# VectorE's share of every dense step queued behind the dot of the latest gather, in issue order alone

## The chip, the cores and the metric

The kernel runs on one core of a Trainium2 chip. The metric is the device time of one execution in microseconds, as the median of several runs. The core has a matrix engine (TensorE, rows call it PE), a vector engine (VectorE, DVE), an engine for activation functions (ScalarE, ACT), GpSimd (POOL), which here only issues the gathers, and a queue engine (SyncE, SP), which here issues all plain loads. 16 DMA engines move the data of all queues.

## The reference, cut to what matters

Two layers over one sequence of 512 tokens with 1024 features. Each layer first mixes tokens, then looks up experts:

```
m  = x @ w_in                                  # q, k, v, LRU branch, gates
ya = DiffAttention(q, k, v); yr = RG-LRU(conv4(xr)) * gelu(gr)
x  = LayerNorm(alpha * x + (g0 * (ya @ w_br_attn) + g1 * (yr @ w_br_lru)) @ w_out)
q  = x @ peer_wq                               # 8 heads, two halves each
s  = q . subkeys;  top 16 of 128 in each half; top 16 of the sums -> 16 expert numbers e per head
act = gelu(x . peer_u[e]);  x = LayerNorm(alpha * x + sum_e g[e] * act[e] * peer_v[e])
```

So every token fetches 8 x 16 = 128 experts per layer, each with a row of `peer_u` and a row of `peer_v`.

## The kernel before

**Tiling.** The 512 tokens are four blocks of 128, one token per partition. The host puts `peer_u` and `peer_v` side by side, so that one expert is a row of 2048 floats. A *gather* (line 819) is one indirect DMA by POOL that brings one expert for each of the 128 tokens of a block: a tile `uvt` of 128x2048 floats, 1.05 MB. A block needs 128 gathers, and there are 2 layers x 4 blocks x 128 = 1024. They land in 8 buffers (pool `gather`).

**What each gather needs (`experts`).** VectorE multiplies the first half of `uvt` with the block's rows `xn` and sums: the *dot* (line 822, one instruction of 128x1024 with an accumulator). For each pair of gathers ScalarE takes the GELU of two dots (`q`, line 829) and VectorE multiplies by the routing weights (`w`, line 784). Then the second half of `uvt`, scaled by `w`, is added to the block's sum: either by VectorE (`acc`, line 790) or by ScalarE and TensorE (a diagonal matrix `dg`, line 794, and two matmuls into `pv`, line 796). Which of the two is settled for each gather when the program is written, by an account of each engine's load (`Load`); 346 of the 1024 go to VectorE. Only after that sum is the buffer free for the gather eight places later.

**Dense work.** Everything else is written by two more streams, `dense()` and `late()`. The list `PLAN` has four entries, each for two blocks of a layer: (layer 0, blocks 0 and 1), (layer 0, blocks 2 and 3), (layer 1, blocks 0 and 1), (layer 1, blocks 2 and 3). An entry has a *mixer* (projections, attention, LRU, merges, output projection, layer norm) and then a *route* (`route`, line 673): scores for 16 half-heads (`score`), the top 16 of each for both blocks (`top16`, lines 716 to 721, VectorE alone), and the choice of 16 experts per head (`choose`, lines 723 to 771, nearly all VectorE) for the first of the two blocks. The choices for the second block come in `late()` (`route_late`, line 697). `choose` works on groups of two heads and ends with the write of 32 columns of expert numbers (`e`, line 761), which the gathers of those heads need.

**The order in which it is written.** `run` (line 841) takes one step at a time from the stream that lies furthest back, on a scale counted in gathers: `PLAN` says that, for example, the route of (layer 1, blocks 2 and 3) is to be written between gathers 730 and 786 and the late choices between 786 and 880. A stream can also wait for another (`wants`): a gather is not written before its route, and a mixer of layer 1 not before its blocks' experts.

**The order in which it is issued.** The program is traced in this written order, but a list scheduler then sets the order on each engine: among the instructions of an engine that it holds for ready, the one written earlier goes first; where that one is not ready by its reckoning, a later one goes ahead. Each engine then executes its own list strictly in that order. So dense work on VectorE can be issued many gathers ahead of the place at which it was written.

Of the kernel before, what the change touches and what calls it, by code (L numbers as in the profile page):

```python
# [18 lines left out]
ALU = mybir.AluOpType  # L19
# [3 lines left out]
D = 1024  # L23
# [97 lines left out]
class Decoder:  # L121
# [652 lines left out]
    def experts(self, l, b, G=2):  # L774
        nc, pp = self.nc, self.pp
        x = self.xn[b]
        pv = None
        e, g = self.e[b], self.g[b]
        began = [False]

        def finish(j0, q, uvs):

            w = pp.tile([P, G], F32, name="w", tag="w")
            nc.vector.tensor_tensor(w, q, g[:, j0 : j0 + G], ALU.mult)  # L784
            for i in range(G):
                j, t = j0 + i, uvs[i]
                self.load.update()
                vector = self.load.dve + 1.22 <= self.load.pe + 1.72
                if j == P - 1 or (vector and j < P - 2):
                    nc.vector.scalar_tensor_tensor(out=acc, in0=t[:, D:], scalar=w[:, i : i + 1],  # L790
                                                   in1=acc, op0=ALU.mult, op1=ALU.add)
                else:
                    dg = pp.tile([P, P], F32, name="dg", tag="dg")
                    nc.scalar.activation(dg, self.ident, AF.Copy, scale=w[:, i : i + 1])  # L794
                    for half in range(2):
                        nc.tensor.matmul(pv[:, half], dg,  # L796
                                         t[:, D + half * 512 : D + (half + 1) * 512],
                                         start=not began[0], stop=j == P - 2)
                    began[0] = True
            yield  # L800

        prev = iter(())
        for j0 in range(0, P, G):
            if j0 % TOPK == 0:
                yield ("route", l, b, j0 // TOPK)
                if j0 == 0:
                    if (l, b) == (0, 0):
                        self.load.update()
                        self.load.begin()
                    acc = pp.tile([P, D], F32, name="acc", tag="acc", bufs=1)  # L810
                    nc.scalar.activation(acc, x, AF.Copy, scale=ALPHA)
                    pv = self.ps_v.tile([P, 2, 512], F32, name="pv", tag="pv")
            dots = pp.tile([P, G], F32, name="dots", tag="dots")
            q = pp.tile([P, G], F32, name="q", tag="q")
            uvs = []
            for i in range(G):
                j = j0 + i
                t = self.gp.tile([P, 2 * D], F32, name="uvt", tag="uv")
                nc.gpsimd.indirect_dma_start(  # L819
                    out=t, out_offset=None, in_=self.uv,  # L820
                    in_offset=bass.IndirectOffsetOnAxis(ap=e[:, j : j + 1], axis=0))
                nc.vector.scalar_tensor_tensor(out=t[:, :D], in0=t[:, :D], scalar=1.0, in1=x,  # L822
                                               op0=ALU.mult, op1=ALU.mult,
                                               accum_out=dots[:, i : i + 1])
                uvs.append(t)
                if i == 0:
                    next(prev, None)
                else:
                    nc.scalar.activation(q, dots, AF.Gelu_apprx_tanh)  # L829
                yield 1  # L830
            prev = finish(j0, q, uvs)
        for _ in prev:
            pass
        sums = pp.tile([P, 1], F32, name="sums2", tag="sums2")
        nc.vector.scalar_tensor_tensor(out=x, in0=acc, scalar=1.0,
                                       in1=pv.rearrange("p a c -> p (a c)"), op0=ALU.mult,
                                       op1=ALU.add, accum_out=sums)
        self.layer_norm(l, 1, [(b, sums)], LN_EPS, acc)
        self.done.add(("experts", l, b))

    def run(self):
        nc = self.nc
        self.setup()
        self.cst = [None] * DEPTH
        self.done = set()
        self.load = Load(nc)

        def gathers():
            for l in range(DEPTH):
                for b in range(NB):  # L850
                    yield from self.experts(l, b)
# [28 lines left out]
        streams = [gathers(), dense(), late()]  # L880
# [3 lines left out]
        while any(live):  # L884
            free = [i for i in range(3) if live[i] and (wants[i] is None or wants[i] in self.done)]
            i = min(free, key=lambda i: (at[i], -i))
            wants[i] = None
            c = next(streams[i], None)
            if c is None:
                live[i] = False  # L890
            elif isinstance(c, tuple):
                wants[i] = c
            elif i:
                at[i] = c
            else:
                at[0] += c
# [34 lines left out]
```

## Time and profile before

| | us |
|---|---|
| median of 3 runs (3443.23 to 3445.84) | 3445.73 |
| the profiled execution, its own time | 3443.5 |
| its span, first to last instruction | 3441.3 |
| first gather issued (line 819) | 300.1 |
| last dot starts (line 822) | 3422.2 |
| PE busy | 2962.3 |
| VectorE busy | 2660.9 |
| ACT busy | 1242.6 |

The first 300 us are the mixer and the first route of layer 0, blocks 0 and 1; nothing is gathered there. Then all 1024 gathers follow, with the rest of the dense work beside them. 1285.92 MB are read in all, 1073.81 MB of them by the gathers. The rate at which the DMA engines move data, in GB/s per stretch of the span, is the line to read first; beside it stand the busy time of each engine and the granted clock of TensorE (PEclk, as a share of full speed).

### The profile page before, as it was taken

To read this page: it belongs to the slowest core of one execution; us is meant where nothing else is said; L and a number is where in the kernel's file an instruction comes from. 1 tells how busy PE (TensorE), PEld (TensorE's weight loads), DVE (VectorE), ACT (ScalarE), POOL (GpSimd) and SP (SyncE) were. 2 spreads that over 40 slices of the span, in tenths; PEclk is the share of its full clock that TensorE was granted. 3 is DMA by queue.
4 is the path that set the end of the run, shared out by engine and by line. 5 is a ranking of instruction groups with operands and counts; after the bars stand their busy time and mean duration, and the time that the engine had idled before them with its cause. 6 is when DMAs were issued, how large, how long until landed. Compare 5 with 4: busy or idle time off the path is not lost.

```text
span 3441.3 us, 38208 instructions
## 1 busy us (share of the span) xinstructions
PE 2962.3 (86%) x11832; PEld 1899.5 (55%) x11832; DVE 2660.9 (77%) x6622; ACT 1242.6 (36%) x2851; POOL 1307.3 (38%) x1033
## 2 busy tenths in 40 slices
PE   8997999999997899999996799999998687656655
PEld 8896666777763466677763366666755232212111
DVE  7765989887689577867699569777679965777776
ACT  7852356652122364633122236644122221111111
POOL 0001334444333434434333433433433344565553
PEclk9998999999999999999997999999999799877677
DMA  5455899999999999999998999999999899999997
GB/s 202 155 174 204 332 408 397 414 418 418 418 398 354 380 392 401 393 417 412 418 389 342 412 393 391 401 413 419 418 412 353 312 405 421 421 422 410 421 422 317
DMA packets 219114, 1290.54 MB, mean 375 GB/s; under 512 B 24593, under 2 KB 37137, under 8 KB 87841
## 3 DMA queue, kind: packets, MB, share of 16 engines
q0 software_dynamic: 147456, 1073.81, 77.0%
q1 hardware_dynamic: 71456, 214.30, 16.4%
q8 instruction: 96, 1.57, 0.2%
q14 instruction: 106, 0.86, 0.1%
HBM read 1285.92 MB, written 2.10 MB: 374 GB/s over the span
## 4 chain that ended last, share of the span: by engine, by line
PE 44%; DVE 24%; DMA 19%; issue 6%; POOL 3%; ACT 3%; POOLq 0%; SPq 0%; DVEq 0%; ACTq 0%
DMA uvt<-uv_dram,e 19%; PE ps_mm L253 18%; PE pv L796 16%; DVE uvt L822 8%; POOL uvt L819 3%; DVE acc L790 3%; PE ps_mm L275 3%; PE ps_ln L313 1%; PE ps_qk L253 1%; DVE oh L756 1%; DVE ef L758 1%; PE s L386 1%; DVE oh L753 1%; PE ps_mm L656 1%; PE po L417 1%
## 5 line engine op out<-in xcount | busy, mean ns | idle before, releaser
L819 POOL DMA_INDIRECT uvt<-uv_dram,e x1024 | 1304.7, 1274 | 2101.5 <-PE pv L796 655.1
L796 PE MATMUL pv<-uvt,dg 128*128 128x512 f32 x2712 | 1417.4, 662 | 379.3 <-ACT dg L794 377.8
L822 DVE SCALAR_TENSOR_TENSOR uvt<-uvt,xn 128x1024 f32<-128x1024 f32 x1024 | 1243.8, 1220 | 248.3 <-DMA uvt<-uv_dram,e 244.4
L796 PEld LDWEIGHTS pv<-uvt,dg 128*128 128x128 f32 x2712 | 527.8, 206 | 1094.7 <-ACT dg L794 604.4
L253 PE MATMUL ps_mm<-room_xT,w 128*128 128x256 f32 x2304 | 538.6, 380 | 0.7 <-ACT room_xT L285 0.7
L829 ACT ACTIVATE q<-dots 128x2 f32<-128x2 f32 x512 | 104.1, 203 | 1132.3 <-DVE uvt L822 1117.4
L253 PEld LDWEIGHTS ps_mm<-room_xT,w 128*128 128x128 f32 x2304 | 430.4, 190 | 108.8 <-issue 53.9
L790 DVE SCALAR_TENSOR_TENSOR acc<-uvt,w,acc 128x1024 f32<-128x1024 f32 x346 | 443.6, 1282 | 7.9
L794 ACT ACTIVATE dg<-ident,w 128x128 f32<-128x128 f32 x678 | 257.4, 398 | 290.3 <-DVE w L784 171.1
L784 DVE TENSOR_TENSOR w<-q,g 128x2 f32<-128x2 f32 x512 | 80.7, 158 | 208.9 <-ACT q L829 203.9
L656 PE MATMUL ps_mm<-room_xT,w 128*128 128x256 f32 (+1 forms) x1056 | 241.5, 377 | 0.0
L656 PEld LDWEIGHTS ps_mm<-room_xT,w 128*128 128x128 f32 x1056 | 194.7, 194 | 42.7 <-issue 19.9
L829 ACT ACT_TABLE_LOAD x115 | 147.5, 1283 | 19.6 <-DVE uvt L822 17.0
L238 DVE TENSOR_TENSOR wsp<-raw,wsp 128x1024 fp32r<-128x1024 f32 x80 | 97.1, 1222 | 27.0 <-ACT wsp L237 24.8
L275 PEld LDWEIGHTS ps_mm<-w,room_xT 128*128 128x128 f32 x768 | 90.8, 192 | 8.5 <-issue 7.1
L275 PEld LDWEIGHTS ps_mm<-w,room_m 128*128 128x128 f32 x768 | 89.2, 192 | 9.2 <-issue 8.4
L275 PE MATMUL ps_mm<-w,room_xT 128*128 128x128 f32 x768 | 92.6, 275 | 0.0
L253 PE MATMUL ps_mm<-room_yr,w 128*128 128x256 f32 x384 | 90.1, 380 | 0.0
L253 PE MATMUL ps_mm<-room_ya,w 128*128 128x256 f32 x384 | 89.5, 379 | 0.0
L275 PE MATMUL ps_mm<-w,room_m 128*128 128x128 f32 x768 | 89.3, 275 | 0.0
L237 ACT CAST wsp<-raw 128x1024 fp32r<-128x1024 f32 x80 | 82.7, 1052 | 14.8 <-PE ps_mm L253 7.8
L822 DVE DVE_READ_ACCUMULATOR uvt<-uvt,xn 128x1 f32 x1024 | 84.1, 82 | 0.0
(196 smaller groups left out, 2980.7 us busy)
## 6 DMA issues: line engine op xcount, KB each, us to landing
w<-wpk_dram SPq DMA_DIRECT2D x304, 512.0 KB
raw<-wpk_dram SPq DMA_DIRECT2D x80, 512.0 KB
uvt<-uv_dram,e POOLq DMA_INDIRECT x1024
gw<-gpk_dram SPq DMA_DIRECT2D x32, 128.0 KB
sk<-spk_dram SPq DMA_DIRECT2D x64, 64.0 KB
xn<-x_dram SPq DMA_DIRECT2D x4, 512.0 KB
out_dram<-xn SPq DMA_DIRECT2D x8, 256.0 KB
lq<-lqk_dram SPq DMA_DIRECT2D x2, 128.0 KB
```

The costliest lines, as they stand in the source:

```text
L237: self.nc.scalar.copy(hi, raw)
L238: self.nc.vector.tensor_tensor(lo, raw, hi.bitcast(F32), ALU.subtract)
L253: self.nc.tensor.matmul(ps[:, :n], w, x, start=i == 0, stop=i == len(steps) - 1)
L275: self.nc.tensor.matmul(out[:, i], x(slice(i * P, (i + 1) * P)), w, start=j == 0, stop=j == len(steps) - 1)
L656: nc.tensor.matmul(pq[:, :n], w[:, kc, :], self.acts_x.plain[:, kc, t0 : t0 + n], start=kc == 0, stop=kc == KC - 1)
L784: nc.vector.tensor_tensor(w, q, g[:, j0 : j0 + G], ALU.mult)
L790: nc.vector.scalar_tensor_tensor(out=acc, in0=t[:, D:], scalar=w[:, i : i + 1], in1=acc, op0=ALU.mult, op1=ALU.add)
L794: nc.scalar.activation(dg, self.ident, AF.Copy, scale=w[:, i : i + 1])
L796: nc.tensor.matmul(pv[:, half], dg, t[:, D + half * 512 : D + (half + 1) * 512], start=not began[0], stop=j == P - 2)
L819: nc.gpsimd.indirect_dma_start(out=t, out_offset=None, in_=self.uv, in_offset=bass.IndirectOffsetOnAxis(ap=e[:, j : j + 1], axis=0))
L822: nc.vector.scalar_tensor_tensor(out=t[:, :D], in0=t[:, :D], scalar=1.0, in1=x, op0=ALU.mult, op1=ALU.mult, accum_out=dots[:, i : i + 1])
L829: nc.scalar.activation(q, dots, AF.Gelu_apprx_tanh)
```

## The change

The dot's instruction is kept in `self.dot`, so that it always names the dot of the last gather written so far. When `run` takes a step from `dense()` or `late()`, it does so inside `issue_after(self.dot)`: every VectorE instruction that the step writes may be issued only after that dot has been issued. It is a matter of order on VectorE's list alone: no semaphore, no wait for the dot to finish, nothing on the other engines. Before the first gather there is no dot, and nothing is tied. The gathers' own stream (dots, `w`, `acc`, the layer norm behind the experts) is not tied either. The written order, the choice between `acc` and `pv` and all arithmetic are the same.

```diff
--- before.py
+++ after.py
@@ -819,9 +819,9 @@
                 nc.gpsimd.indirect_dma_start(
                     out=t, out_offset=None, in_=self.uv,
                     in_offset=bass.IndirectOffsetOnAxis(ap=e[:, j : j + 1], axis=0))
-                nc.vector.scalar_tensor_tensor(out=t[:, :D], in0=t[:, :D], scalar=1.0, in1=x,
-                                               op0=ALU.mult, op1=ALU.mult,
-                                               accum_out=dots[:, i : i + 1])
+                self.dot = nc.vector.scalar_tensor_tensor(
+                    out=t[:, :D], in0=t[:, :D], scalar=1.0, in1=x, op0=ALU.mult, op1=ALU.mult,
+                    accum_out=dots[:, i : i + 1]).ins
                 uvs.append(t)
                 if i == 0:
                     next(prev, None)
@@ -843,6 +843,7 @@
         self.setup()
         self.cst = [None] * DEPTH
         self.done = set()
+        self.dot = None
         self.load = Load(nc)
 
         def gathers():
@@ -885,7 +886,12 @@
             free = [i for i in range(3) if live[i] and (wants[i] is None or wants[i] in self.done)]
             i = min(free, key=lambda i: (at[i], -i))
             wants[i] = None
-            c = next(streams[i], None)
+            if i and self.dot is not None:
+
+                with self.tc.issue_after(self.dot):
+                    c = next(streams[i], None)
+            else:
+                c = next(streams[i], None)
             if c is None:
                 live[i] = False
             elif isinstance(c, tuple):
```

What that does to VectorE's list can be counted in dots. In the list of before, the dense instructions of each route stand 20 to 48 dots ahead of the place at which they were written (late ones of the last entry 56 to 100), those of the mixers of the last three entries mostly 4 to 17; in the new list all dense instructions stand 0 to 6 dots behind it. In the first mixer that runs beside gathers (written at gathers 32 to 150), the two lists hardly differ: there before is 0 to 3 dots ahead on average. The four writes of `e` in a route stand behind these dots:

| route of | before | with the change | first gather that needs it |
|---|---|---|---|
| layer 0, block 2 | 211, 223, 233, 241 | 234, 245, 256, 267 | 256, 288, 320, 352 |
| layer 1, block 0 | 448, 457, 469, 479 | 484, 497, 510, 523 | 512, 544, 576, 608 |
| layer 1, block 2 | 708, 719, 730, 740 | 744, 757, 770, 783 | 768, 800, 832, 864 |
| layer 1, block 3 (late) | 744, 749, 753, 757 | 802, 820, 839, 857 | 896, 928, 960, 992 |

The order of POOL's gathers and of SP's loads is the same, but for the place of two stores among the loads. TensorE's and ScalarE's lists change in many places, since the scheduler reckons with the later VectorE work.

VectorE before, at dots 711 and 712, where the route of layer 1, blocks 2 and 3 is issued (`sv`, `si`, `top`: the values and places of the top 16; `sc`: scores; `xn_103` and `g_113`: rows and weights of block 1, whose gathers run here):

```order
L822 SCALAR_TENSOR_TENSOR uvt,dots<-uvt,xn_103 128x1024
L716 MAX sv<-sc 128x8
L716 MAX top_17922<-sc 128x8
L718 MAX_INDEX si<-sv,sc 128x8
L718 MAX_INDEX top_17923<-top_17922,sc 128x8
L721 MATCH_REPLACE sc<-sv,sc 128x128
L822 SCALAR_TENSOR_TENSOR uvt,dots<-uvt,xn_103 128x1024
L716 MAX sv<-sc 128x8
L721 MATCH_REPLACE sc<-top_17922,sc 128x128
L784 TENSOR_TENSOR w<-q,g_113 128x2
L718 MAX_INDEX si<-sv,sc 128x8
L790 SCALAR_TENSOR_TENSOR acc<-uvt,w,acc 128x1024
```

With the change the same gathers have this around them, row after row, from dot 711 on:

```order
L822 SCALAR_TENSOR_TENSOR uvt,dots<-uvt,xn_103 128x1024 x2
L784 TENSOR_TENSOR w<-q,g_113 128x2
L790 SCALAR_TENSOR_TENSOR acc<-uvt,w,acc 128x1024
L822 SCALAR_TENSOR_TENSOR uvt,dots<-uvt,xn_103 128x1024 x2
L784 TENSOR_TENSOR w<-q,g_113 128x2
L790 SCALAR_TENSOR_TENSOR acc<-uvt,w,acc 128x1024
L822 SCALAR_TENSOR_TENSOR uvt,dots<-uvt,xn_103 128x1024 x2
L784 TENSOR_TENSOR w<-q,g_113 128x2
L790 SCALAR_TENSOR_TENSOR acc<-uvt,w,acc 128x1024
L822 SCALAR_TENSOR_TENSOR uvt,dots<-uvt,xn_103 128x1024 x2
L784 TENSOR_TENSOR w<-q,g_113 128x2
```

The steps of the route have left the stretch between these dots: between two dots only `w` and `acc` of the gathers themselves are left.

VectorE before, in the late choices of layer 1, block 3, at dots 746 to 749 (`oh`, `ef`: the one-hot product that looks up the chosen expert's number; `e_111`: expert numbers of block 3):

```order
L753 TENSOR_TENSOR oh<-iota,pf 128x864 x2
L822 SCALAR_TENSOR_TENSOR uvt,dots<-uvt,xn_103 128x1024
L784 TENSOR_TENSOR w<-q,g_113 128x2
L756 TENSOR_TENSOR oh<-oh,ca 128x864 x2
L822 SCALAR_TENSOR_TENSOR uvt,dots<-uvt,xn_103 128x1024
L758 TENSOR_REDUCE ef<-oh 128x16
L784 TENSOR_TENSOR w<-q,g_113 128x2
L758 TENSOR_REDUCE ef<-oh 128x16
L822 SCALAR_TENSOR_TENSOR uvt,dots<-uvt,xn_103 128x1024
L761 CAST e_111<-ef 128x32
```

With the change the same steps stand in the gathers of block 2 (`xn_4375`, `g_114`), at dots 797 to 802:

```order
L753 TENSOR_TENSOR oh<-iota,pf 128x864
L822 SCALAR_TENSOR_TENSOR uvt,dots<-uvt,xn_4375 128x1024
L784 TENSOR_TENSOR w<-q,g_114 128x2
L822 SCALAR_TENSOR_TENSOR uvt,dots<-uvt,xn_4375 128x1024
L756 TENSOR_TENSOR oh<-oh,ca 128x864
L822 SCALAR_TENSOR_TENSOR uvt,dots<-uvt,xn_4375 128x1024
L784 TENSOR_TENSOR w<-q,g_114 128x2
L822 SCALAR_TENSOR_TENSOR uvt,dots<-uvt,xn_4375 128x1024
L758 TENSOR_REDUCE ef<-oh 128x16
L822 SCALAR_TENSOR_TENSOR uvt,dots<-uvt,xn_4375 128x1024
L761 CAST e_111<-ef 128x32
```

A choice of two heads lay within four or five dots; now each of its large steps has a dot or two to itself, and a whole choice has 18.

## Rows read from the trace of the kernel before

**Rows 1.** Page, part 2: GB/s in 40 equal slices of the span.

```profile
GB/s 202 155 174 204 332 408 397 414 418 418 418 398 354 380 392 401 393 417 412 418 389 342 412 393 391 401 413 419 418 412 353 312 405 421 421 422 410 421 422 317
```

**Rows 2.** Stretches: us, busy (instructions) of each engine, PEclk, DMA share, GB/s.

```profile
core 0: us, PE busy (x) PEld busy (x) DVE busy (x) ACT busy (x) POOL busy (x), PEclk, DMA share, GB/s
...
946.00:1204.00 258.00, 216.87 (x673) 123.06 (x672) 208.93 (x695) 72.51 (x192) 98.83 (x80) 0.93 0.96 377
1204.00:1462.00 258.00, 248.26 (x980) 162.94 (x980) 200.39 (x519) 156.37 (x330) 99.18 (x80) 0.97 0.99 395
...
1720.00:1892.00 172.00, 136.73 (x455) 82.21 (x454) 166.33 (x600) 41.74 (x120) 64.55 (x50) 0.89 0.94 366
...
2064.00:2322.00 258.00, 253.67 (x1092) 173.34 (x1091) 214.53 (x471) 154.74 (x317) 102.17 (x84) 1.00 1.00 402
...
2580.00:2752.00 172.00, 122.87 (x347) 64.81 (x346) 171.90 (x618) 45.67 (x115) 61.83 (x50) 0.87 0.90 332
...
2838.00:3354.00 516.00, 320.38 (x503) 106.72 (x501) 372.17 (x607) 73.26 (x232) 286.30 (x206) 0.79 1.01 420
```

**Rows 3.** Waits of PE, then of POOL, 2580 to 2752 us: total us, times, longest.

```profile
PE pv L796 <- ACT dg L794: 44.6, 19, 5.4
...
POOL uvt L819 <- PE pv L796: 38.1, 16, 6.3
```

**Rows 4.** VectorE's groups by line, 2580 to 2752 us: busy us, mean ns.

```profile
L822 DVE SCALAR_TENSOR_TENSOR uvt<-uvt,xn 128x1024 f32<-128x1024 f32 x52 | 63.0, 1212 | 0.0
L790 DVE SCALAR_TENSOR_TENSOR acc<-uvt,w,acc 128x1024 f32<-128x1024 f32 x14 | 17.8, 1272 | 0.0
```

**Rows 5.** The gathers' own instructions on VectorE, whole run: busy us, mean ns.

```profile
L822 DVE SCALAR_TENSOR_TENSOR uvt<-uvt,xn 128x1024 f32<-128x1024 f32 x1024 | 1243.8, 1220 | 248.3 <-DMA uvt<-uv_dram,e 244.4 <-PE pv L796 2.8 <-issue 0.2
...
L822 DVE DVE_READ_ACCUMULATOR uvt<-uvt,xn 128x1 f32 x1024 | 84.1, 82 | 0.0
L784 DVE TENSOR_TENSOR w<-q,g 128x2 f32<-128x2 f32 x512 | 80.7, 158 | 208.9 <-ACT q L829 203.9 <-issue 3.3 <-ACT dg L794 1.3
```

**Rows 6.** A route's instructions on VectorE, whole run, by shape: busy us, mean ns.

```profile
L758 DVE TENSOR_REDUCE ef<-oh 128x16 f32<-128x864 f32 x64 | 66.5, 1045 | 0.1
L753 DVE TENSOR_TENSOR oh<-iota,pf 128x864 f32<-128x864 f32 x64 | 66.4, 1052 | 1.3 <-PE po L417 1.0
L718 DVE FIND_INDEX8 si<-sv,sc 128x8 uint32<-128x128 f32 x128 | 35.8, 283 | 0.0
L716 DVE MAX8 sv<-sc 128x8 f32<-128x128 f32 x128 | 34.7, 282 | 25.4 <-ACT sc L670 23.7 <-ACT dg L794 1.0 <-issue 0.6
L718 DVE FIND_INDEX8 pi<-tv,ca 128x8 uint32<-128x54 f32 x128 | 25.5, 208 | 0.0
L716 DVE MAX8 tv<-ca 128x8 f32<-128x54 f32 x128 | 22.4, 205 | 0.0
L721 DVE MATCH_REPLACE8 sc<-sv,sc 128x128 f32<-128x128 f32 x64 | 17.3, 273 | 0.0
L721 DVE MATCH_REPLACE8 ca<-tv,ca 128x54 f32<-128x54 f32 x64 | 12.3, 199 | 0.0
L736 DVE TENSOR_TENSOR ca<-fi 128x16 f32<-128x16 f32 x64 | 10.8, 169 | 0.0
L718 DVE MATCH_VALUE_LOAD si<-sv,sc 128x8 f32 x128 | 9.7, 76 | 0.1
```

**Rows 7.** Page, part 6: loads of a route's step, KB each.

```profile
w<-wpk_dram SPq DMA_DIRECT2D x304, 512.0 KB
...
sk<-spk_dram SPq DMA_DIRECT2D x64, 64.0 KB
```

**Rows 8.** Stretch of the first mixer beside gathers, columns as in group 2.

```profile
516.00:688.00 172.00, 171.19 (x760) 119.92 (x757) 153.80 (x360) 106.67 (x222) 74.54 (x58) 1.00 1.00 406
```

**Rows 9.** VectorE's longest waits, 430 to 860 us: total us, times, longest.

```profile
DVE uvt L822 <- DMA uvt<-uv_dram,e: 23.6, 19, 2.5
```

**Rows 10.** VectorE's longest waits, 2838 to 3354 us: total us, times, longest.

```profile
DVE uvt L822 <- DMA uvt<-uv_dram,e: 105.2, 118, 1.8
```

## The prediction, made before the changed kernel ran

> **What bounds the kernel now.** I read the rate of the DMA engines first, since 1.07 of the 1.29 GB are gathers. Where nothing but gathers runs, from 2838 to 3354 us, the rate is 420 GB/s for 516 us on end, with VectorE busy 372 us of these and TensorE 320; 206 gathers are issued there, 2.50 us for each [rows 2]. That is the ceiling of this kernel. The reader should now look for where the rate is lower although gathers were wanted [rows 1]. There are three dips, and in each the dense work of a route is being issued: 946 to 1204 us at 377 GB/s, 1720 to 1892 at 366, 2580 to 2752 at 332 [rows 2]. Against 420 they are short by 258 x (1 - 377/420) = 26.4 us, 172 x (1 - 366/420) = 22.1 us and 172 x (1 - 332/420) = 36.0 us, together 84.5 us. In the third VectorE is busy 171.9 of 172 us, in the second 166.3, in the first 208.9 of 258; TensorE has 13 to 30 per cent idle in them [rows 2]. The waits say how a full VectorE reaches the DMA: TensorE's sum over the experts waits for the scaled diagonal, which waits for VectorE's dots and weights (44.6 us in the third dip), and POOL waits for these matmuls until a buffer is free (38.1 us) [rows 3]. So the dips are bound by VectorE, the gather-only stretches by the DMA. Between them lie the mixers, at 395 and 402 GB/s (short by 15.4 and 11.1 us over 258 us each), where TensorE is busy 248 and 254 of 258 us [rows 2].
>
> **The change, part by part.** It adds no instruction and no semaphore. It moves dense VectorE work to later places; the part on the change counts by how many dots.
>
> *The price of a route.* One half-head of one block (`top16`) costs 2 x 0.282 + 2 x (0.283 + 0.076) + 0.273 + 0.076 = 1.63 us, the last term the load of match values, taken as for line 718. A group of two heads has eight of them (four half-heads, two blocks): 13.0 us. A choice for two heads has six one-hot steps of 1.05 us, two times 2 x 0.205 + 2 x (0.208 + 0.076) + 0.199 + 0.076 = 1.25 us for the top 16 of candidates, ten sums of 0.169 us and eight small ones that I price like those: 11.9 us. Together 24.9 us a group [rows 6]. A gather's own part is dot and accumulator 1.30 us and half a `w`, 0.08 us [rows 5]; in the third dip 14 of 52 gathers were summed by VectorE at 1.27 us [rows 4], which makes 1.72 us; in the route stretches of the changed list only 4 of 44 or of 52, so 1.5 us.
>
> *How full VectorE is.* The third dip holds some 3.5 groups and 2.5 late choices (by the places of the writes of `e`) and 52 dots: 3.5 x 24.9 + 2.5 x 11.9 + 52 x 1.72 = 206 us of durations in 172 us. Instructions overlap at their ends, so a sum is to be divided by 1.2 to become time. There 50 gathers were issued, one per 3.44 us.
>
> *With the change* a group takes 11 dots in the first route beside gathers and 13 in the other two, against 10 to 11 before, and the late choices of the last entry take 18 dots in place of four. VectorE then needs (11 x 1.5 + 24.9)/1.2/11 = 3.14 us per gather in the first and (13 x 1.5 + 24.9)/1.2/13 = 2.85 in the others. The DMA needs 2.50 us plus the group's loads, four `w` of 512 KB and four `sk` of 64 KB [rows 7], 2.36 MB or 5.6 us at 420 GB/s: 3.01 and 2.93 us per gather. So the first route stays short by 44 x 0.13 = 5.7 us, and the others become bound by the DMA. Of 84.5 us, 78.8 are to be had. I don't take all: with VectorE and DMA this close together some is lost. The nearest row is the first mixer beside gathers, 516 to 688 us, with VectorE 89 and TensorE 99 per cent busy at 406 GB/s, 3.3 per cent short [rows 8]. On 148 route gathers of 2.95 us, 437 us, that is 15 us. 64 remain.
>
> *What the tie costs.* On VectorE's list dense work now stands behind a dot that may wait for its landing, and cannot slip past it; behind the dense work stand the next dots, and TensorE's next dense matmul waits for it, with sums over experts queued behind that matmul. The first mixer beside gathers shows such a list, since both lists are nearly alike there: over 430 us and some 142 gathers VectorE waited 23.6 us for landings, 0.17 us per gather [rows 9]. The mixers of the last two entries run beside some 288 gathers (272 to 416 and 528 to 672). Ends: nothing, since VectorE has 44 to 58 us idle in their 258 [rows 2]; or all of 288 x 0.17 = 49 us on the path. I take half, 24 us, because VectorE has the room but TensorE has next to none.
>
> *Moved at no cost.* POOL's list is the same, and SP's as well but for two stores. The weight loads come later with the steps that free their buffers, into stretches that had none; the bytes stay. Each first write of `e` in a route stands 22 to 28 dots ahead of the gather that needs it, and the buffers reach 8 ahead, so no gather waits for its route; past that cover each dot of delay would cost 2.5 us. ScalarE's new list hides in the 40 per cent or more that it idles [rows 2]. The first 300 us hold no dot and stay.
>
> *Sum.* 64 - 24 = 40 us less. The profiled execution took 3443.5 us, so 3403.5; the median of the runs lies 2.2 us above it, so 3406.
>
> A figure of the Trainium skill speaks against this sum: "DMA: Bandwidth & Descriptors", under Specifications, gives some 358 GB/s as a core's share of its memory. By that figure only the third dip, at 332, would be short, by 172 x (1 - 332/358) = 12.5 us. The trace disagrees, with 420 GB/s for 516 us; no sum here uses the page.
>
> **The rivals.**
>
> *Lockstep (slower).* In the last two mixers TensorE has no slack, and its dense matmuls now wait for VectorE steps that are held back until the dot before them has its data. For: the wait for landings is 0.51 us per gather where VectorE has little to do (105.2 us over 206 gathers) [rows 2, 10], and the tie forbids filling it with dense work. Against: 0.17 in the one mixer with such a list [rows 9]. On 288 gathers the wait eats the 64 us from 0.22 us per gather on. At 0.34, midway between the two rows, it costs 98 us: 3443.5 - 64 + 98 + 2 = 3480.
>
> *The dips move with the routes (same).* If single steps between dots that wait don't overlap, the sums aren't divided by 1.2: 3.76 us per gather in the first route, 3.42 in the others, against 3.01 and 2.93. That is 44 x 0.75 + 104 x 0.49 = 84 us short again, all that was to be won: 3446. For: short dense pieces now stand alone between dots. Against: the overlap is at the ends of any two instructions, dots too, and the late choices of the last entry surely leave the dip.
>
> *The mixers gain too (faster still).* There the old list floods TensorE with dense work; the new one spreads it. If the tie costs nothing and the 15.4 and 11.1 us go as well [rows 2], 64 + 26 = 90 us: 3356. Against: TensorE's work there is the same, and it is nearly full in both lists.
>
> *The page's ceiling.* A memory limit below 420 GB/s that hits the mixed stretches alone would leave 12.5 us to win, 3433. For it speak the 395 and 402 GB/s of the mixers, against it the full TensorE there [rows 2].
>
> That the tie does nothing can be ruled out: the new list shows it.
>
> **How the numbers follow.** A measurement of this kernel can tell some 0.2 per cent, 7 us, from no change. Chances: the forecast 0.58 (3383 with a free tie to 3432 with its full price), lockstep 0.18, dips that move 0.12, mixers too 0.10, the page 0.02. Most likely 3406. The range leaves out most of lockstep and the edges: from 3362, short of the best case, to 3457, where dips that move and half a price of the tie meet. Faster by over 0.2 per cent: forecast 0.56, mixers 0.10, page 0.02 and 0.02 of moved dips, 0.70. Within: 0.10, mostly moved dips. Slower: 0.20, lockstep and a part of the moved dips.
>
> **What the profile of the changed kernel would show.** Right: no stretch of 86 us after 500 us and before the end below 385 GB/s; VectorE nowhere full for 172 us; the late choices of the last entry at 18 dots, inside stretches at 420 GB/s; VectorE's waits for landings in the last two mixers up by 20 to 60 us in all, TensorE's idle time there likewise. Wrong: a dip below 360 GB/s at the new place of a route with VectorE full there (the dips moved), or mixers below 385 GB/s with TensorE waiting for VectorE (lockstep). The prediction fails on its price if the mixers' gathers wait over 0.22 us each, and on its gain if a route's VectorE time per gather stays above 3.2 us.

## The result, and the profile after

| | before | after |
|---|---|---|
| median, us (4 runs of each, side by side) | 3445.78 (3443.23 to 3446.22) | 3398.66 (3394.51 to 3402.74) |
| the profiled execution, us | 3443.5 | 3394.5 |
| its span, us | 3441.3 | 3392.8 |
| VectorE busy, us | 2660.9 | 2665.2 |
| TensorE (PE) busy, us | 2962.3 | 2947.0 |

After over before is 0.9865, 95% interval 0.9848 to 0.9882: 47 us less. The forecast was 3406, 40 us less. The total is nearly the one foreseen, but the two terms that make it were both wrong, in opposite directions. The rest of this text is about that.

Page of the changed kernel, part 2, GB/s in 40 slices (before: [rows 1]):

```profile
GB/s 198 155 176 200 315 408 401 407 418 419 418 407 405 347 410 408 415 418 419 419 402 412 391 397 413 409 412 412 418 419 409 385 345 421 421 422 405 422 422 318
```

The dips have not gone; they have become narrower. Stretches of the changed kernel, 86 us each, columns as in [rows 2]:

```profile
1032.00:1118.00 86.00, 73.39 (x237) 43.44 (x238) 78.90 (x300) 22.93 (x69) 32.66 (x27) 0.90 1.00 398
1118.00:1204.00 86.00, 76.57 (x221) 42.16 (x219) 76.59 (x324) 29.24 (x67) 27.62 (x26) 0.90 0.89 347
1892.00:1978.00 86.00, 77.55 (x225) 41.46 (x224) 79.36 (x306) 31.17 (x76) 34.49 (x29) 0.94 0.96 383
2666.00:2752.00 86.00, 75.83 (x223) 41.18 (x222) 74.89 (x284) 24.59 (x67) 29.19 (x27) 0.90 0.85 334
```

Against 420 GB/s the last three are short by 86 x 73/420 = 14.9, 7.6 and 17.6 us, 40 us in all, where the (wider) dips of [rows 2] were short by 84.5. VectorE is busy 87 to 92 per cent in them, not full.

**The same gathers side by side.** Slices of time hold other work in the two kernels, so from here on stages are cut at dots: 160, 288, 416, 544, 672 and 800. The first, third and fifth stage hold the three routes, the second and fourth the last two mixers. Stretches of the kernel before:

```profile
841.00:1257.00 416.00, 368.13 (x1385) 231.97 (x1384) 316.45 (x948) 114.70 (x291) 154.70 (x128) 0.95 0.98 391
1257.00:1665.00 408.00, 398.22 (x1611) 274.97 (x1610) 303.06 (x679) 190.46 (x423) 162.29 (x128) 0.98 1.00 405
1665.00:2067.00 402.00, 340.38 (x1215) 201.24 (x1213) 311.45 (x927) 109.30 (x285) 150.06 (x128) 0.93 0.97 388
2067.00:2471.00 404.00, 398.64 (x1697) 279.20 (x1696) 325.04 (x677) 196.24 (x416) 158.64 (x128) 1.00 1.01 408
2471.00:2862.00 391.00, 313.70 (x1012) 170.14 (x1011) 321.57 (x983) 95.78 (x252) 151.59 (x128) 0.91 0.96 376
```

and of the changed one:

```profile
841.00:1246.00 405.00, 363.30 (x1367) 231.30 (x1366) 315.72 (x938) 106.28 (x280) 154.87 (x127) 0.95 0.98 396
1246.00:1642.00 396.00, 381.96 (x1537) 258.42 (x1536) 309.74 (x720) 193.94 (x426) 162.08 (x130) 1.00 1.01 415
1642.00:2029.00 387.00, 346.66 (x1279) 214.18 (x1278) 305.73 (x893) 105.20 (x277) 158.88 (x128) 0.95 0.99 403
2029.00:2428.00 399.00, 383.35 (x1635) 264.98 (x1634) 331.40 (x710) 195.47 (x417) 171.35 (x129) 0.99 1.01 413
2428.00:2812.00 384.00, 327.18 (x1145) 193.14 (x1143) 297.64 (x866) 83.55 (x242) 156.08 (x129) 0.93 0.97 393
```

2021 us have become 1971; nothing happened outside (the 841 us ahead are the same, the gather-only end too). Three things are to be seen. The routes are 33 us shorter (1209 to 1176) and TensorE's idle time in them, the stretch less its first figure, fell from 187 to 139 us. The mixers are 17 us shorter (812 to 795). And TensorE does 32 us less in the mixers (797 to 765), where it had been full but for 15 us, and 15 us more in the routes.

In the prediction's measure, the time above the 420 GB/s ceiling (length x (1 - rate/420)), the routes go from 100 to 64 us and the mixers from 26 to 11.

### The profile page after: what moved, and what is told of

Read it like the earlier page. It is cut to its first block, busy times and chain, and to the rows that moved or that the text cites. A ratio compares the mean times of both kernels' runs of the same rounds, so it can differ in the third digit from the quotient of the medians.

```text
span 3392.8 us, 38229 instructions
## 1 busy us (share of the span) xinstructions
PE 2947.0 (87%) x11832; PEld 1899.8 (56%) x11832; DVE 2665.2 (79%) x6622; ACT 1229.6 (36%) x2840; POOL 1319.6 (39%) x1033
## 4 chain that ended last, share of the span: by engine, by line
PE 47%; DMA 22%; DVE 16%; issue 6%; ACT 5%; POOL 3%; SPq 0%; POOLq 0%; DVEq 0%; ACTq 0%
DMA uvt<-uv_dram,e 21%; PE pv L796 18%; PE ps_mm L253 15%; DVE uvt L822 6%; PE ps_mm L275 4%; PE ps_mm L656 4%; POOL uvt L819 3%; DVE acc L790 2%; PE ps_ln L313 1%; PE s L386 1%; PE ps_qk L253 1%; PE po L417 1%; PE ps_sc L663 1%; PE pg L489 1%; DVE ef L758 1%
## 5 line engine op out<-in xcount | busy, mean ns | idle before, releaser
L532 ACT ACTIVATE mth<-ps_mm 128x256 f32<-128x256 f32 x64 | 24.5, 382 | 181.6 <-PE ps_mm L253 181.5
L253 PEld LDWEIGHTS ps_mm<-room_ya,w 128*128 128x128 f32 x384 | 71.6, 190 | 32.0 <-ACT mth L532 13.1
```

What stands on the lines that cost most here:

```text
L253: self.nc.tensor.matmul(ps[:, :n], w, x, start=i == 0, stop=i == len(steps) - 1)
```

## The experiments

Every kernel was timed against the kernel before on the same chip. For each the table gives the time above the ceiling by stage (the first mixer stage is dots 0 to 160; worked out from the bytes of all DMA records of the stage at 420.5 GB/s), and, for dots 160 to 800: how long VectorE stood at a dense instruction whose input another engine had not delivered (summed from the waits of VectorE, without dots, `w` and block sums), the mean time from a gather's issue to the start of its dot, and that from the end of its dot until POOL issues the gather eight places later, which takes over its buffer. All but the first two columns are in us and are worked out from the trace of one execution, which lay up to 7 us from the median (tie_late 3435.7, the change 3394.5).

| kernel | median us | ratio to before, 95% | first mixer | routes | mixers | VectorE at dense inputs | issue to dot | dot to reissue |
|---|---|---|---|---|---|---|---|---|
| before | 3445 | | 32 | 102 | 27 | 174 | 17.4 | 6.6 |
| the change | 3398.7 | 0.9848 to 0.9882 | 33 | 65 | 12 | 72 | 15.9 | 7.5 |
| tie_route | 3418.9 | 0.9909 to 0.9936 | 34 | 69 | 28 | 148 | 16.4 | 7.2 |
| tie_mixer | 3448.6 | 0.9997 to 1.0015 | 31 | 97 | 30 | 90 | 16.9 | 7.1 |
| tie_late | 3428.6 | 0.9938 to 0.9963 | 36 | 84 | 29 | 159 | 17.3 | 6.5 |
| lead16 | 3432.0 | 0.9947 to 0.9973 | 32 | 87 | 27 | 159 | 17.1 | 6.8 |
| shift | 3423.0 | 0.9914 to 0.9947 | 50 | 79 | 7 | 79 | 15.1 | 8.3 |
| before_noacc | 3450.7 | 1.0009 to 1.0026 | 33 | 105 | 26 | 205 | 17.3 | 6.8 |
| dup_after | 3423.1 | 0.9917 to 0.9947 | 43 | 77 | 18 | 54 | 15.8 | 7.8 |
| dup_before | 3476.6 | 1.0078 to 1.0110 | 44 | 117 | 31 | 189 | 17.6 | 6.7 |
| before_nomr | 3434.4 | 0.9948 to 0.9975 | 36 | 91 | 27 | 187 | 17.2 | 6.7 |
| after_nomr | 3387.0 | 0.9817 to 0.9843 | 31 | 52 | 21 | 73 | 15.9 | 7.4 |
| tie_pe | 3504.2 | 1.0154 to 1.0182 | 49 | 132 | 34 | 162 | 14.9 | 9.7 |
| tie_two | 3490.3 | 1.0106 to 1.0142 | 48 | 122 | 34 | 113 | 14.8 | 9.7 |

### Parts of the change, and a looser tie

tie_route, the tie for the routes and the late choices alone (`self.part` is set to "route" while a route is written, else to "mixer"):

```diff
-            if i and self.dot is not None:
+            if self.dot is not None and (i == 2 or i == 1 and self.part == "route"):
```

> Only the routes and the late choices are tied to the latest dot; the mixers may run ahead on VectorE as before. Theory A (the gain is VectorE work of routes spread over more dots): at least 30 us of the 47 us stay, 3405 to 3417 us, and the mixer stretches (dots 288 to 416 and 544 to 672) take as long as before, 408 and 404 us. Theory B (the gain is the mixers' pacing, since with the tie they no longer flood TensorE): at most 20 us, above 3425 us. My prediction priced the tie of the mixers as a loss of 24 us; by that this kernel is faster than the full change, near 3375.

tie_mixer, the tie for the mixers alone:

```diff
-            if i and self.dot is not None:
+            if self.dot is not None and i == 1 and self.part == "mixer":
```

> Only the mixers are tied; routes and late choices may run ahead once their mixer is done. Theory A: 0 to 20 us less than before (3426 to 3446), the dips at the routes stay with VectorE full in them. Theory B: 30 us or more less, below 3416. By the price in the prediction (a loss of 24 us): 3470.

tie_late, for the late choices alone:

```diff
-            if i and self.dot is not None:
+            if i == 2 and self.dot is not None:
```

> Only the late choices are tied. In the old list three of them stood in the third dip, 3 x 11.9 / 1.2 = 30 us of VectorE. Theory A: the third dip loses 10 to 20 us, 3426 to 3436; the other two dips stay. Theory B: no change, 3440 to 3446.

lead16, all of it tied, but to the dot of 16 gathers earlier:

```diff
+            back = self.dots[-16 - 1] if len(self.dots) > 16 else None
...
-                with self.tc.issue_after(self.dot):
+                with self.tc.issue_after(back):
```

> Everything is tied as in the change, but to the dot 16 gathers before the latest, so dense VectorE work may run 16 dots ahead. Theory A: the routes, which ran 20 to 48 ahead, still spread, and the mixers get back their lead of 4 to 17: equal to the change or better, 3375 to 3405. If the tight pacing itself is what gains (theory B): worse than the change, 3415 to 3440.

The routes' tie is worth 26.5 us, near theory A and far from the 3375 of the prediction's price, and the late choices make 17 of these. A lead of 16 gathers costs 33 of the change's 47 us. The mixers' tie alone is worth nothing (3 us, inside the interval of no change), and with the routes' tie beside it it brings 20 us more (3418.9 to 3398.7): the two don't add up, and the loss that the prediction charged to the mixers' tie is seen in none of the runs. The two mixers and the last route with the mixers' tie alone:

```profile
1250.00:1652.00 402.00, 383.14 (x1532) 258.50 (x1531) 304.81 (x689) 195.54 (x428) 166.28 (x129) 0.99 1.00 406
...
2052.00:2456.00 404.00, 387.63 (x1625) 266.25 (x1626) 327.06 (x678) 203.28 (x424) 167.70 (x129) 0.98 1.00 404
2456.00:2861.00 405.00, 331.80 (x1150) 193.97 (x1149) 325.75 (x994) 97.09 (x256) 153.98 (x129) 0.93 0.94 374
```

TensorE's work has left the mixers here too (383 and 388 us), but in the last route, which took up 18 us of it, TensorE idles 73 us (405 - 332), about the 77 of before, and the stage grows from 391 to 405 us: more than the 6 us that the two mixers saved. With the routes tied as well that stage does 327 us of TensorE work in 384. That taking up the work made the stage longer is read from these rows and not shown: the route ahead of it took up 12 us as well (340 to 352) and did not grow.

### Is it the place of the block's end?

In the changed kernel each of the three remaining dips lies where a block of 128 gathers ends inside a route. shift moves the three later routes 16 to 20 gathers ahead:

```diff
-    (0, [2, 3], 30, 222, 270, 370),
-    (1, [0, 1], 270, 470, 526, 620),
-    (1, [2, 3], 526, 730, 786, 880),
+    (0, [2, 3], 30, 206, 254, 370),
+    (1, [0, 1], 256, 454, 510, 620),
+    (1, [2, 3], 512, 710, 766, 880),
```

> The change, with the three later routes moved 16 to 20 gathers ahead in the list of due times (they end at gathers 254, 510 and 766 in place of 270, 526 and 786), so that the end of a block of gathers (256, 512, 768) falls behind the route and not into it. Theory C (what is left of the dips is a route and a block's end at once): the time above the DMA ceiling in the three stretches around them, 64 us in the change, falls by 25 to 40 us, 3360 to 3375. Rival (VectorE is simply at its limit during a route, wherever it lies): no gain, 3392 to 3405. Rival (the mixers before it, squeezed by as many gathers, pay it back): 3400 to 3420.

It failed: the first mixer, squeezed into fewer gathers, lost 17 us, and the routes lost 14 in place of winning; only the later mixers won, 5. (The account of loads also gave VectorE 20 sums more, 366.) Around the ends of the three blocks, whose next blocks' first dots start at 1165, 1963 and 2758 us (the routes' last expert numbers at 1155, 1952 and 2747):

```profile
1118.00:1204.00 86.00, 67.86 (x177) 35.14 (x176) 71.69 (x264) 33.10 (x72) 28.47 (x26) 0.88 0.88 337
...
1978.00:2064.00 86.00, 82.79 (x353) 56.65 (x352) 63.44 (x151) 44.74 (x92) 33.20 (x26) 1.00 0.94 360
...
2666.00:2752.00 86.00, 72.70 (x194) 36.12 (x192) 76.00 (x302) 24.21 (x65) 33.70 (x30) 0.94 0.92 356
2752.00:2838.00 86.00, 69.66 (x144) 27.83 (x144) 63.38 (x156) 23.65 (x60) 44.05 (x36) 0.94 0.99 405
```

A dip stays at the first end and follows the second, where the route is over. At the third the low stretch lies ahead of the block's end, in the route. So neither the route nor the block's end is shown to be what makes a dip.

### Is it VectorE's time?

The prediction held the dips for VectorE's time. One run and two pairs ask that. before_noacc takes 49 of the 346 sums off VectorE, in the three dips alone:

```diff
+                at = (l * NB + b) * P + j
+                vector = vector and not any(a <= at < a + 54 for a in (192, 432, 704))
```

> The kernel before, with no tie, but in the three stretches of its dips (gathers 192 to 245, 432 to 485, 704 to 757) VectorE sums no expert: some 50 of its 1.27 us sums go to ScalarE and TensorE. Theory A (the dips are VectorE's time): 50 x 1.27 / 1.2 = 53 us of VectorE gone from stretches that were short by 84 us: 3390 to 3425. Rival (the dips come from the chain through TensorE, whose work rises by 50 x 1.7 us there): 3440 to 3480.

Its three dips, which were at 377, 366 and 332 GB/s with VectorE busy 209, 166 and 172 us [rows 2]:

```profile
946.00:1204.00 258.00, 228.13 (x709) 127.90 (x708) 190.86 (x677) 74.73 (x203) 88.71 (x78) 0.95 0.95 371
1720.00:1892.00 172.00, 162.31 (x548) 97.42 (x548) 133.50 (x521) 44.71 (x138) 60.29 (x52) 0.97 0.98 383
2580.00:2752.00 172.00, 141.86 (x424) 77.26 (x422) 157.00 (x616) 48.26 (x130) 57.83 (x51) 0.95 0.90 340
```

VectorE is no longer full in any; one dip is better by 17 GB/s, one by 8, and one is worse by 6. But the sums went to TensorE, so this run alone proves little. dup_after and dup_before do a first one-hot step twice, 63 and 62 times. They add not only that: the account of loads answers by moving 15 of the 346 sums to ScalarE and TensorE, so VectorE's busy time rises by 42 and 38 us (2707.6 and 2698.9 on their pages). dup_after's edit (dup_before has it with a condition that holds from nearly the same place, since it knows no `self.dot`):

```diff
+            if self.dot is not None:
+                nc.vector.tensor_tensor(oh, self.iota.unsqueeze(1).to_broadcast(sh),
+                                        pf[:, h].unsqueeze(2).to_broadcast(sh), ALU.is_equal)
```

> The change, with the first one-hot step (line 753, 1.05 us of VectorE) done twice wherever gathers run, 63 more of them; the result is the same. The account of loads moves 15 sums off VectorE in answer. By the prices of the prediction: two more per group make 3.30 us per gather in the first route (limit 3.01) and 2.98 in the others (2.93), 44 x 0.16 + 104 x 0.05 = 12 us more, none in the late choices: 3405 to 3415. If the routes have slack left with the tie: 3395 to 3402. If every microsecond of VectorE counts: 63 x 1.05 / 1.2 = 55 us more, 3450.

> The kernel before with the same doubled step, 62 more. Theory A (its dips are VectorE's time): the 14 groups and 3 late choices that lie in the three dips pay in full, some 30 x 1.05 / 1.2 = 26 us and a few for the rest: 3465 to 3480, at least 10 us more than the same doubling costs with the tie. Rival (VectorE does not bind them): 3440 to 3455.

The doubled steps, 65 us of durations less the sums moved, cost 24 us with the tie and 32 without; the first mixer, whose list is nearly the same in both, takes 10 to 13 of either. Outside it, in routes and mixers together, the cost is 18 us with the tie and 20 without (unrounded). So VectorE's work does cost time with either list: 3476.6 lies in the range of dup_before's theory A, and its rival (VectorE does not bind them) failed. (3423.1 lies in none of dup_after's three ranges.) But the expected difference of 10 us or more, that the tie makes such work cheap, isn't there. The opposite test leaves the `match_replace` steps out, with each gather's sum kept on the engine that it had (`KEPT`, a fixed list of one bit per gather):

```diff
-                if j == P - 1 or (vector and j < P - 2):
+                vector = KEPT[(l * NB + b) * P + j] == "1"
+                if vector:
...
-            if o.start == 0:
+            if o.start == 0 and ("route", 0, 0, 1) not in self.done:
```

> The kernel before, with the MATCH_REPLACE steps of the routes left out from the first gather on (about 150 of them, 0.36 us each with the load of match values, 54 us of VectorE's durations; the second eight of every top 16 then repeat the first eight, so the output is another) and with every gather's sum on the engine that had it in the kernel before, so that TensorE's work stays as it was. Theory V, the route dips are VectorE's time: the doubled one-hot step put 65 us on and cost 21 us outside the first mixer, so 54 us less should give 15 to 25 us: 3420 to 3430, with the three dips above 385, 375 and 350 GB/s. Rival, the dips are something else (TensorE's flood, the end of a block): within 7 us of 3445.

> The changed kernel with the same steps left out and its own choices of engine kept. Theory V, the tie has moved most of this work to where VectorE has room: less is won than on the kernel before, 5 to 12 us, 3387 to 3394. If as much is won as on the kernel before, the tie did not make VectorE's work cheaper, and its gain lies elsewhere.

There were 182 steps, not 150 (VectorE has 364 instructions fewer, each step with its load of match values). The two pages' rows of busy time, before and before_nomr:

```profile
PE 2962.3 (86%) x11832; PEld 1899.5 (55%) x11832; DVE 2660.9 (77%) x6622; ACT 1242.6 (36%) x2851; POOL 1307.3 (38%) x1033
```

```profile
PE 2964.9 (86%) x11832; PEld 1903.6 (55%) x11832; DVE 2619.2 (76%) x6258; ACT 1245.7 (36%) x2854; POOL 1296.6 (38%) x1033
```

VectorE's busy time is 41.7 us less, and the time 10.8 us less, between the two theories; on the changed kernel the time is 11.7 us less. So a microsecond of VectorE taken out is worth about a quarter of one over the whole run, and the same with either order, while one put in cost 0.6 to 0.8 (24 by 42, 32 by 38). Such a run also gets new lists: in the route stages alone 10 and 13 us were won, and the first mixer of the one kernel and the later mixers of the other gave 5 and 9 us back. The third dip, 2580 to 2752 us, is not better at all in before_nomr (its stage, dots 672 to 800, takes 392 us, before 391):

```profile
2580.00:2752.00 172.00, 126.98 (x339) 65.57 (x338) 165.22 (x546) 48.67 (x118) 64.37 (x51) 0.82 0.86 323
```

Less VectorE work did not raise its rate. By these pairs the change did not win by making VectorE's work cheaper. That VectorE's time has no part in the gain is not shown: tie_late took 24 us of it out of the third route stage (321.57 to 297.12) and put it beside the gathers behind, and the stage became 14 us shorter (391 to 377):

```profile
2474.00:2850.90 376.90, 311.37 (x1051) 173.17 (x1050) 297.12 (x858) 87.06 (x241) 150.18 (x127) 0.95 0.98 393
```

### Is it TensorE's order?

tie_pe puts the tie on TensorE in place of VectorE, behind the last expert matmul (`pv`) written so far; tie_two ties each engine's instructions, VectorE's behind the dot and TensorE's behind that matmul. The edit of tie_pe:

```diff
+                        self.mm = nc.tensor.matmul(pv[:, half], dg,
...
+                with self.tc.issue_after(self.mm):
+                    c = next(streams[i], None)
```

> The kernel before, with TensorE's part of every dense step tied behind the last matmul of a sum over the experts that the program has ahead of it, and VectorE's part free. Theory M, the mixers gain because TensorE's dense work no longer runs ahead of the sums: the last two mixers gain 10 to 15 us as with the change, the routes gain as far as the scores that VectorE waits for come later: 3395 to 3415. Theory V alone: the mixers stay and only the routes gain, 3415 to 3435. Rival, a dense matmul held back costs TensorE its filling: 3445 and more.

> The changed kernel with TensorE's tie as well, both engines' parts of a dense step behind the program's last gather. Theory M: the gain of both, 3385 to 3396. Theory V: TensorE's dense work follows VectorE's anyway, within 7 us of 3399. Rival, TensorE and VectorE in lockstep: 3410 and more.

Both are slower than either kernel, 3504.2 and 3490.3 us, as only the last rival of each allowed. In these two a dot starts earliest of all kernels after its gather's issue (14.9 and 14.8 us), but its buffer comes free latest (9.7 us after the dot). POOL's wait for the expert matmuls, whole run, before and in tie_pe (total us, times, longest):

```profile
POOL uvt L819 <- PE pv L796: 655.1, 352, 10.4
```

```profile
POOL uvt L819 <- PE pv L796: 994.3, 418, 17.1
```

Worked out from the records for dots 160 to 800, 2.6 us go by from the end of a `dg` to its first matmul in tie_pe, in place of 0.9 before and 1.5 with the change. TensorE's idle time ahead of dense matmuls is no longer than before (33 us, before 48); ahead of the sums it is (195, before 153). So the sums stand behind dense matmuls that run, not behind ones that wait: it is not the lockstep of the prediction's first rival. An order by written place as such is not what helps; it helps on VectorE and harms on TensorE.

## Why the total was right and its terms were not

**What moved.** VectorE's waits, longest first, between dots 160 and 800. Before, 841 to 2862 us:

```profile
DVE w L784 <- ACT q L829: 146.3, 151, 7.5
DVE uvt L822 <- DMA uvt<-uv_dram,e: 112.6, 101, 2.5
DVE mth L535 <- PE ps_mm L253: 28.5, 16, 2.6
DVE room_m L535 <- PE ps_mm L253: 27.4, 14, 5.5
DVE hist L477 <- ACT xr L475: 18.2, 6, 4.3
DVE pr L390 <- PE s L386: 17.6, 13, 5.6
DVE thx L507 <- ACT thx L490: 13.3, 5, 3.3
DVE sv L716 <- ACT sc L670: 13.2, 9, 3.5
```

After, 841 to 2812 us:

```profile
DVE w L784 <- ACT q L829: 179.3, 174, 5.8
DVE uvt L822 <- DMA uvt<-uv_dram,e: 135.4, 120, 2.6
DVE sm_st L765 <- ACT ef L764: 15.4, 13, 3.6
DVE xn L585 <- PE ps_mm L275: 12.0, 9, 2.2
DVE mu L501 <- ACT mu L499: 11.7, 9, 2.3
DVE pr L390 <- PE s L386: 7.7, 8, 1.9
```

The reader should see what is missing below. In the old list a dense step stood as far ahead as the scheduler put it, often ahead of its input: VectorE stood at `mth` and `room_m` until TensorE had the projection, at `sv` until ScalarE had the scores, while gathered rows lay behind it. With the change `mth`, `hist`, `thx` and `sv` have left the list of waits and `room_m` has all but left it: the waits at dense inputs fall from 174 to 72 us in all. (Of these 102 us, 56 come back as longer waits for `q` and for landings.) Behind the dot of the written place the input is mostly there. The Trainium skill says of these queues, in "PSUM — Partial Sum Buffer", section Engine vs sequencer instructions, that ScalarE's, VectorE's and GpSimd's are strict FIFO; these rows agree, with up to 5.5 us for one such stand.

These waits are not the whole of it. By stage, 76 of the 102 us lie in the two mixers, which became 17 us shorter, and 27 in the three routes, which became 33 us shorter. tie_route shortens the route stages by 30 us (1209 to 1179) with only 9 us less of such waits in them, and tie_late the third one by 14 with none less. We read it so that the dots gain there because less dense work stands ahead of them, whether it waits or runs. Both would show in one figure: how long rows that had landed lay until their dot started (a gather is counted as landed when the packets of all gathers up to it have ended). It was 7.3 us before and is 4.9 with the change; in tie_route it is 4.7 in the routes and 7.8 in the mixers.

What the gathers got from it stands in the table's last columns: 1.5 us less from issue to dot, 0.9 us more from dot to reissue. With eight buffers the net of 0.64 us (unrounded) is 0.64/8 = 0.08 us per gather, 51 us over 640 gathers, where the stretches above gave 50. (The two must agree: the two figures and the dot itself add up to the time between two issues into one buffer.) The amounts of VectorE's work hardly touch the first figure (17.2 to 17.6 for the four kernels with the old order and more or less work, 15.8 to 15.9 for the three with the new), the order does. But an early dot is not enough, since the buffer must also come free: tie_pe and tie_two have the earliest dots and are the slowest. And the link from the waits to the time is a correlation with exceptions: tie_mixer takes 84 of the 102 us of waits away and is not faster, shift takes 95 away and is 24 us slower than the change.

**Point by point.**

- *The ceiling.* Right: 421 and 422 GB/s in the gather-only slices after 2838 us, but for one at 405 (before, one at 410).
- *"The dips are bound by VectorE."* Wrong as a price. (TensorE's idle share in the three dips, by the way, is 16 to 29 per cent by [rows 2], not 13 to 30.) VectorE was full in the third dip, but full is not the same as limiting: 41.7 us of its work taken out are worth 11. The Trainium skill's "Perfetto Trace Analysis", Identifying the Most-Contended Engine, has the same rule, to find the engine with the highest share of busy time and improve it first. In the third dip that is VectorE, and the measurement goes against it there: the dip stayed at 323 GB/s with part of VectorE's work taken out.
- *The routes give back 64 us.* The failed step is "the others become bound by the DMA", with all but 15 us of 78.8 to be had. Measured: 37 (102 to 65). VectorE's time per gather in the first route is under the limit that was set (1032 to 1204 us: 155.5 us for 53 gathers, 2.93), and the DMA still is not full: the dips around the block ends remain, 40 us in the three slices above.
- *The tie costs 24 us in the mixers.* The sign is wrong: they win 15. The wait that was priced did come. Waits for landings in the two mixers, first before (1257 to 1665 us, 2067 to 2471), then after (1246 to 1642, 2029 to 2428):

```profile
DVE uvt L822 <- DMA uvt<-uv_dram,e: 0.4, 1, 0.4
```

```profile
DVE uvt L822 <- DMA uvt<-uv_dram,e: 0.3, 1, 0.3
```

```profile
DVE uvt L822 <- DMA uvt<-uv_dram,e: 28.8, 30, 2.4
```

```profile
DVE uvt L822 <- DMA uvt<-uv_dram,e: 1.4, 2, 1.0
```

  From 0.7 to 30.2 us: within the 20 to 60 of the prediction, and TensorE's idle time there rose from 15 to 30, as it said. But half of such waiting was charged to the path, 24 us, and little of it can have been there: 28.8 of the 30.2 us lie in the first of the two mixers, which is only 396 x 5/420 = 5 us above the ceiling. A dot that waits for its landing is an engine that is ahead of the DMA. And TensorE's work in these stages fell by 32 us. That its work "there is the same" was the argument against the rival that the mixers gain too; it was not the same. The rival had its mechanism, spreading, right. So that the total of 40 us came out near the measured 47 is luck: 27 us too much for the routes and 39 too little for the mixers largely cancel.
- *Lockstep.* Did not come. The waits for landings in the two mixers are 30.2 us over 256 gathers, 0.12 each, under its threshold of 0.22 (and they rose to 0.21 over all 640 gathers, from 0.18). What the threshold took them to cost, all of their length, they did not cost.
- *Late choices.* Right, but for the first of the four, which runs beside 406 GB/s (2752 to 2838 us): they are spread out. The last 16 first one-hot steps, half of the route and half of the late choices, before and after:

```profile
L753 DVE TENSOR_TENSOR oh<-iota,pf x16: 1032/1051/1060, 2581.2 to 2750.7; 128x864 f32<-128x864 f32 x16
```

```profile
L753 DVE TENSOR_TENSOR oh<-iota,pf x16: 1046/1054/1059, 2640.9 to 2941.8; 128x864 f32<-128x864 f32 x16
```

  They take 301 us in place of 170, into the stretch at 421 GB/s. The late choices' tie alone gives 17 us (tie_late).
- *The signs.* "No stretch below 385" failed (347, 383, 334). "VectorE nowhere full for 172 us" held. The sign for moved dips, below 360 GB/s with VectorE full, was half met: below 360, VectorE not full.

**What is left at a block's end.** Stretches of 10 us in the changed kernel, around the end of the block at gather 256:

```profile
1140.00:1150.00 10.00, 6.96 (x21) 3.46 (x19) 9.42 (x18) 5.06 (x11) 2.95 (x3) 0.91 1.00 388
1150.00:1160.00 10.00, 8.17 (x11) 3.01 (x11) 7.85 (x37) 5.85 (x9) 2.58 (x3) 0.58 0.86 306
1160.00:1170.00 10.00, 8.62 (x23) 5.21 (x22) 8.87 (x31) 2.09 (x6) 0.40 (x2) 0.66 0.41 166
```

and from its timeline (start, us, engine, line; in brackets the idle time before it and what ended it):

```profile
1152.58 6.61 PE L796 MATMUL pv<-uvt,dg 128*128 128x512 f32 x8 [1.83 <-ACT dg L794]
...
1156.63 1.11 POOL L819 DMA_INDIRECT uvt<-uv_dram,e  x1 [4.68 <-PE pv L796]
...
1161.13 1.28 DVE L342 SCALAR_TENSOR_TENSOR xn<-xn,ln_st,ps_ln 128x1024 f32<-128x1024 f32 x1 [2.50 <-PE ps_ln L313]
```

The old block's last sum and layer norm take VectorE, ScalarE and TensorE, the new block's sums start with matmuls of 0.83 us each (6.61/8), and POOL waits for them. That this chain is the rest of the loss was only read from these rows; the one run that touched it (shift) moved the routes away from it and did not win.

**What stays open.** Why the mixers gain only with the routes tied: that the routes must have room for TensorE's work is argued from its busy time and not shown. TensorE's own list changed too, since the scheduler reckons with the later VectorE work (136 matmuls fewer in the two mixers); no run tied VectorE with TensorE's list held as it was, so the two can't be told apart. Whether a lead between 0 and 16 gathers would be better still was not run. No kernel of these that computes the whole result beats the changed one.

## What to carry to other kernels

An engine that executes its list in order is best given work whose input is ready, and little of it ahead of the work that frees a buffer: on VectorE here, tying optional work behind the place where it was written won 47 us and took 102 us of standing at the head of its list away, while such a tie on TensorE cost 59 us. Before an engine at 100 per cent is called the bound, take some of its work out with all else kept: here a microsecond taken out was worth a quarter, and nothing in the dip where the engine was full. And a wait that a change adds is no cost until one knows whose time it takes; the waits for landings grew as foreseen, and the stages that they stand in became shorter.

## What the hardware showed that was not expected

At the block's end TensorE's granted clock is 0.58 and 0.66 over 20 us, so mostly the lower of its two levels, 1.2 GHz, right after 10 us in which it was busy for 6.96. It was back at 1.00 for 1170 to 1180 us. The eight expert matmuls of the timeline above took 0.83 us each there. By line, TensorE's group of these matmuls in the changed kernel, first 1032 to 1118 us, then 1150 to 1180 (busy us, mean ns, idle before):

```profile
L796 PE MATMUL pv<-uvt,dg 128*128 128x512 f32 x89 | 43.9, 641 | 5.2 <-ACT dg L794 5.1
```

```profile
L796 PE MATMUL pv<-uvt,dg 128*128 128x512 f32 x32 | 18.7, 738 | 1.8 <-ACT dg L794 1.8
```

So the slow clock falls on the very matmuls that POOL waits for. The prediction had no term for it. What it costs in all was not measured.
